# Finer gated-row sums, five early down-projection steps, and the second stage's stores on GpSimd's queue, in a one-core hybrid decoder layer

## The chip, the cores and the metric

The kernel runs on one core of one Trainium2 chip. Time is the device time of one execution in microseconds (us). The core has five engines with instruction streams of their own: TensorE (PE; its weight loads are PEld), VectorE (DVE), ScalarE (ACT), GpSimd (POOL) and SyncE (SP). In this kernel DMA transfers are issued by SP and by POOL; each works through its own stream in order.

## The reference

One decoder layer over 2048 tokens of width 1024, all float32: a mixer of two recurrent head groups, then a convolutional feed-forward block with a feed-forward width of 2816, and a final norm. Cut to what matters here:

```python
def _conv_ffn(h, w_up, conv_w, conv_b, w_down):
    u = h @ w_up                                # 1024 -> 5632
    u = lax.conv_general_dilated(u, conv_w[:, None, :], window_strides=(1,),
            padding=[(CONV_WIDTH - 1, 0)], ...) + conv_b     # causal, 3 taps, per column
    gate, val = jnp.split(u, 2, axis=-1)
    return (jax.nn.silu(gate) * val) @ w_down   # 2816 -> 1024

def reference(x, ...):
    ...                                         # h, the two mixers o_hg and o_rw
    x = x + jnp.concatenate([o_hg, o_rw], axis=-1) @ w_out[l]
    x = x + _conv_ffn(_rmsnorm(x, norm2_w[l]), w_up[l], conv_w[l], conv_b[l], w_down[l])
    return _rmsnorm(x, final_norm_w)
```

## The kernel before

**Matmuls.** Every float32 operand is split into a high part (written by ScalarE, a CAST; L245 in `split`) and a low part (the difference, written by DVE; L246). A product is three matmuls: high by high (L261), low by high (L262), high by low (L263). Names ending in h and l are these parts: uraw is a raw up-projection weight and uwh, uwl its parts; draw is a raw operand of the down-projection, and dah, dal, dbh, dbl the parts of its two sides.

**Stages.** Stage 1, up to about 1388 us, holds the input projections and the mixers; the change doesn't touch it. The second stage begins with the output projection of the last of four token blocks (its rows go to the DRAM tensor x1d, L1227). Then come the up-projection, until about 2337 us, and the down-projection, until the end.

**Up-projection** (`run`). It is done for the two halves of the tokens (h = 0, 1; 1024 tokens each) and for 22 pairs of column blocks (NFF = 22), so 44 iterations n. One iteration computes a gate and a value block of 128 columns as a 2x2 block product with seven products instead of eight (the Strassen-Winograd scheme): `prod` issues 12 matmuls of 128x512, seven times. The left operands are the weight quarters and their sums (s1 to s4); the right ones are the blocks Bh, Bl of the normed input and their sums Ts. ScalarE copies intermediate sums (m1, m2, m3), DVE adds and applies the convolution (L1431 to L1440), ScalarE applies the silu and DVE multiplies (L1445). The result y, 128 rows by 1024 tokens, is stored as two 256 KB pieces to the DRAM tensors gd0 and gd1 (first half) or gd2 and gd3 (second half) at L1447. The last two products of an iteration and all that follows (`late`) run inside the next iteration. The last iteration's `late` also calls `down_start`.

**Side work.** Between the products, `aside(n)` takes one entry of a list of small steps per product, not before the iteration that the entry names (`first_at`). The list holds, in this order: the norm of the last two token blocks (`norm_last`, with stores to h2d), the sums Ts of the second half, the sums Tw of the down weights, the sums Sg0 of the rows gd0 and gd1 (g = 0; 11 of them, KH = 11) and eight sums Sg1 of gd2 and gd3 (g = 1; EARLY = 8). Each sum loads four 128x512 tiles into a ring of six buffers (br), does four additions on DVE in place (L1280, L1281 in one step, L1283, L1284 in a second, for the gated rows; L1271 to L1275 for the others) and stores four tiles (L1266). `four` spreads this over five entries: loads, nothing, two operations, two operations and all four stores, nothing.

**Down-projection.** Also 2x2 with seven products, per half g; one step is a pair of 128-row operands and 12 matmuls (`d_matmuls`), and `steps` lists 143 of them. The accumulators are da and db. One product (fa) runs between the two halves of the up-projection and its result waits in M2. `down_start` runs the first three steps with the up-projection's buffers (br and uwh, uwl) inside the last `late`, ahead of the work on the last y, so that TensorE has these 36 matmuls while y and the silu are computed. Then the loop loads four steps ahead (draw, a ring of six tiles, three steps), splits two steps ahead (`take`), and issues the matmuls; some steps also load a tile of x1d (xt3), and steps 13, 19 and 25 call `g_sums` for the three remaining sums Sg1 (sraw, stores at L200). The finished rows go to the output at L1489.

**What sets the order.** Before the change every DMA of the second stage is issued by SP, except for the two stores of the last y, which POOL issues. Within an engine a scheduler orders the instructions by their dependences and by a list of priorities that follows the code, so a step may stand earlier in an engine's order than the code has it. Tiles of a pool are reused in rings, and whoever writes such a tile waits for the last reader.

Of the kernel before, what the change touches and what calls it, by code (L numbers as in the profile page):

```python
# [18 lines left out]
P = 128  # L19
# [42 lines left out]
def tile_layer(ctx, tc, consts, x, norm1_w, w_in, hg_lb_logits, hg_norm_w, rw_shift_mu, rw_w0, rw_w2,  # L62
# [4 lines left out]
    V, S, TE = nc.vector, nc.scalar, nc.tensor  # L67
    dma = nc.sync.dma_start

# [122 lines left out]
    def g_sums(tile_, g, kk):  # L192

        a11, a12, a21, a22 = (tile_(krows(gd_[2 * g + u], q, kk)) for u in range(2) for q in range(2))
        V.tensor_add(a22, a21, a22)
        V.tensor_sub(a21, a11, a21)
        V.tensor_sub(a11, a22, a11)
        V.tensor_sub(a12, a12, a11)
        for i, t_ in enumerate((a22, a11, a21, a12)):
            dma(krows(Sg[g][i], 0, kk), t_)  # L200

# [906 lines left out]
    with ExitStack() as c2:  # L1108
# [36 lines left out]
        with tc.tile_pool(name="op", bufs=1, reuse_waits="tile") as op_:  # L1145
# [52 lines left out]
            for dh in range(2):  # L1198
# [26 lines left out]
                for i in range(4):  # L1225
                    V.tensor_add(xt[i], accs[i], xt[i])
                    dma(x1d[b][i * P:(i + 1) * P, dh * 512:dh * 512 + 512], xt[i])  # L1227


        with tc.tile_pool(name="up", bufs=1, reuse_waits="tile") as up:  # L1230
# [11 lines left out]
            def norm_last(b, i2):  # L1242
# [11 lines left out]
                def evict(k, tp, w):  # L1254
                    t_ = hr.tile([P, 256], F32, tag="br", name="h2", bufs=6)
                    act(t_, tp, AF.Copy, scale=w)
                    dma(h2d[b][k * P:(k + 1) * P, i2 * 256:i2 * 256 + 256], t_)

# [17 lines left out]

            def s_make(ts, part):
                a11, a12, a21, a22 = ts
                if part == 0:
                    V.tensor_add(a22, a21, a22)  # L1280
                    V.tensor_sub(a21, a11, a21)  # L1281
                else:
                    V.tensor_sub(a11, a22, a11)  # L1283
                    V.tensor_sub(a12, a12, a11)  # L1284
# [3 lines left out]
            s_out = lambda row: lambda ts: [(row(i), ts[j]) for i, j in enumerate((3, 0, 2, 1))]  # L1288
            for b in (2, 3):
# [30 lines left out]
            def between():  # L1320
# [10 lines left out]
                for i in range(4):  # L1331
                    t_ = raw_(None)
                    act(t_, accs[i], AF.Copy)
                    dma(M2[i], t_)
                yield
# [8 lines left out]
            def run():  # L1344
# [9 lines left out]
                for n in range(2 * NFF + 1):  # L1354
# [41 lines left out]
                    if late is not None:  # L1396
                        late(end=down_start) if n == 2 * NFF else late()
                    if n == 2 * NFF:
                        break
                    cg = up.tile([P, 16 + 2 * BLK], F32, tag="cg", name="cg", bufs=2)[:, 0:2 + 2 * BLK]  # L1400
# [21 lines left out]
                    def late(h=h, fb=fb, operand=operand, prod=prod, acc_a=acc_a, acc_d=acc_d, a22=a22, a12=a12, cg=cg,  # L1422
# [23 lines left out]
                        for b in range(2):  # L1446
                            (dma if end is None else nc.gpsimd.dma_start)(gd_[2 * h + b][fb * P:(fb + 1) * P, :],  # L1447
                                                                  ys[0][:, b * BLK:(b + 1) * BLK])
# [4 lines left out]
    with tc.tile_pool(name="dn", bufs=1, reuse_waits="tile") as dn:  # L1453
# [10 lines left out]
        raws = {}  # L1464

        def load(s_):
            if s_ < N and s_ not in raws:
                g, p, kk = steps[s_]
                raws[s_] = d_loads(s_, d_raw("draw"))
                if p == 0 and kk in (4, 6, 8, 10) or p == 2 - g and kk in (1, 3, 5, 7):  # L1470
                    u, i = (0, kk // 2 - 2) if p == 0 else (1, kk // 2)
                    t_ = dn.tile([P, D], F32, tag="xt3", name="xt3", bufs=12)
# [32 lines left out]
        accs = {"a": dstate["accs"]}  # L1505
        for s_ in range(3, 7):
            load(s_)
        take(3)
        take(4)
# [3 lines left out]
        for s_ in range(3, N):  # L1513
            g, p, kk = steps[s_]
# [60 lines left out]
```

## Time and profile before

| what | value |
|---|---|
| median of 3 runs | 2748.41 us |
| the three runs | 2748.82, 2748.41, 2739.77 us |
| the profiled execution | 2740.67 us |
| its span, first to last instruction | 2738.9 us |
| granted TensorE clock, mean | 0.989 |
| TensorE busy in the span | 2634.9 us, 96% |
| DVE, ScalarE, GpSimd busy | 69%, 49%, 13% |

The profiled execution is close to the fastest of the runs. Rows of the timeline give the start, the duration, the engine, the line of the code, the operation and "out<-in" tiles; the bracket at the end says how long the engine had been idle and what ended that. SPq are the DMA instructions that SP issues. Rows of waits give the waiting instruction, what it waited for, and the total, the number of times and the longest. A matmul lasts 0.39 us but a new one starts every 0.23 us, since they overlap.

### The profile page before, as it was taken

The page shows a single profiled execution, that of the slowest core. Times are in us where ns is not written, and L with a number is a line of the kernel's source. Part 1 is how long each engine was busy: PE and PEld are TensorE (multiplying, and loading weights), DVE is VectorE, ACT ScalarE, POOL GpSimd, SP SyncE. Part 2 cuts the span into 40 slices and gives each one's busy share as a digit, 9 for nine tenths or more (in the row PEclk, how much of TensorE's full clock was granted, in tenths as well). Part 3 has the DMA queues.
Part 4 walks back from the last instruction along what each step waited for, and adds up shares of the span by engine and source line. Part 5 has one row for each costly group of instructions (what it writes and reads, how often), then busy time and mean ns, then how long its engine had stood idle before and what let it go on. Part 6 is the DMA issues. An engine that isn't in the chain of part 4 may idle for free.

```text
span 2738.9 us, 47949 instructions
## 1 busy us (share of the span) xinstructions
PE 2634.9 (96%) x18059; PEld 2098.9 (77%) x18059; DVE 1896.9 (69%) x3665; ACT 1344.5 (49%) x2168; POOL 367.4 (13%) x660
## 2 busy tenths in 40 slices
PE   7999999989999999999899999999999999999998
PEld 6777777767777767777677788887888877788887
DVE  4857656566556664656667889988898888667556
ACT  5446443444544444334456754556545444445444
POOL 6433222212321113222100000000000000000000
PEclk9999999999999999999999999999999999999999
DMA  8655544355663546844575357746763454888665
GB/s 302 200 159 165 165 138 128 115 152 164 216 189 105 152 137 208 273 142 133 168 260 179 118 197 265 237 151 208 259 223 123 145 185 151 285 303 273 214 193 185
DMA packets 365438, 517.87 MB, mean 189 GB/s; under 512 B 97440, under 2 KB 194070, under 8 KB 365206
## 3 DMA queue, kind: packets, MB, share of 16 engines
q1 hardware_dynamic: 313265, 345.39, 39.3%
q0 software_dynamic: 51872, 169.41, 19.0%
q8 instruction: 142, 2.33, 0.3%
q14 instruction: 91, 0.74, 0.1%
q10 hardware_dynamic: 68, 0.02, 0.0%
HBM read 376.27 MB, written 138.41 MB: 188 GB/s over the span
## 4 chain that ended last, share of the span: by engine, by line
PE 67%; DMA 10%; DVE 10%; issue 6%; ACT 4%; SPq 1%; POOL 1%; DVEq 0%; ACTq 0%; POOLq 0%
PE pj L261 8%; PE pj L262 7%; PE pj L263 7%; PE ua L261 4%; PE ua L263 4%; PE ua L262 4%; PE da L262 2%; PE da L261 2%; PE da L263 2%; PE ud L263 2%; PE ud L261 2%; PE ud L262 2%; PE db L262 2%; PE db L263 2%; PE hg L972 2%
## 5 line engine op out<-in xcount | busy, mean ns | idle before, releaser
L261 PE MATMUL pj<-hh,wh 128*128 128x512 f32 x960 | 403.2, 420 | 2.3 <-ACT hh L117 1.4
L263 PE MATMUL pj<-hh,wl 128*128 128x512 f32 x960 | 380.0, 396 | 0.1
L262 PE MATMUL pj<-hl,wh 128*128 128x512 f32 x960 | 379.1, 395 | 0.0
L261 PE MATMUL ua<-Bh,uwh 128*128 128x512 f32 x704 | 277.0, 393 | 10.4 <-ACT m L117 9.3
L263 PE MATMUL ua<-Bh,uwl 128*128 128x512 f32 x704 | 274.5, 390 | 0.1
L262 PE MATMUL ua<-Bl,uwh 128*128 128x512 f32 x704 | 274.2, 390 | 0.0
L261 PEld LDWEIGHTS pj<-hh,wh 128*128 128x128 f32 x960 | 181.7, 189 | 55.4 <-issue 12.7
L263 PEld LDWEIGHTS pj<-hh,wl 128*128 128x128 f32 x960 | 181.5, 189 | 40.8 <-DMA wl<-Win170l 0.9
L262 PEld LDWEIGHTS pj<-hl,wh 128*128 128x128 f32 x960 | 181.8, 189 | 39.6 <-issue 6.2
L245 ACT CAST uwh<-uraw 128x512 fp32r<-128x512 f32 x220 | 133.2, 616 | 101.5 <-PE ua L262 42.0
L246 DVE TENSOR_TENSOR dal<-draw,dah 128x512 fp32r<-128x512 f32 x140 | 96.7, 690 | 116.0 <-ACT dah L245 115.4
L245 ACT CAST dah<-draw 128x512 fp32r<-128x512 f32 x140 | 87.1, 622 | 169.9 <-PE da L262 81.6
L246 DVE TENSOR_TENSOR uwl<-uraw,uwh 128x512 fp32r<-128x512 f32 x220 | 146.8, 686 | 31.3 <-ACT uwh L245 31.1
L261 PEld LDWEIGHTS ua<-Bh,uwh 128*128 128x128 f32 x704 | 132.2, 188 | 41.8 <-ACT m L117 14.0
L263 PEld LDWEIGHTS ua<-Bh,uwl 128*128 128x128 f32 x704 | 132.2, 188 | 28.7 <-DVE uwl L246 1.0
L262 PEld LDWEIGHTS ua<-Bl,uwh 128*128 128x128 f32 x704 | 132.3, 188 | 26.6
L261 PE MATMUL ud<-Bh,uwh 128*128 128x512 f32 x352 | 137.8, 391 | 0.0
L263 PE MATMUL ud<-Bh,uwl 128*128 128x512 f32 x352 | 137.1, 389 | 0.0
L262 PE MATMUL ud<-Bl,uwh 128*128 128x512 f32 x352 | 137.0, 389 | 0.0
L261 PE MATMUL da<-dbh,dah 128*128 128x512 f32 x340 | 131.2, 390 | 3.4 <-ACT dbh L245 3.4
L262 PE MATMUL da<-dbl,dah 128*128 128x512 f32 x340 | 132.5, 390 | 0.5 <-DVE dbl L246 0.5
L263 PE MATMUL da<-dbh,dal 128*128 128x512 f32 x340 | 132.1, 389 | 0.0
(570 smaller groups left out, 6049.5 us busy)
## 6 DMA issues: line engine op xcount, KB each, us to landing
uraw<-in_w_up_dram SPq DMA_DIRECT2D x176, 256.0 KB, 3.2
woraw<-in_w_out_dram POOLq DMA_DIRECT2D x96, 256.0 KB, 3.6
br<-gd SPq DMA_DIRECT2D x90, 256.0 KB, 4.4
draw<-Sg SPq DMA_DIRECT2D x88, 256.0 KB, 3.2
draw<-Tw SPq DMA_DIRECT2D x88, 256.0 KB, 3.5
gd<-y SPq DMA_DIRECT2D x86, 256.0 KB, 3.0
Sg<-br SPq DMA_DIRECT2D x76, 256.0 KB, 2.5
xt<-x1d SPq DMA_DIRECT2D x32, 512.0 KB, 6.7
```

The lines of the kernel that those rows point to most:

```text
L245: S.copy(hi, src)
L246: V.tensor_sub(lo, src, hi.bitcast(F32))
L261: TE.matmul(acc, lh, rh, start=first, stop=False, skip_group_check=skip)
L262: TE.matmul(acc, lh, rl, start=False, stop=False, skip_group_check=skip)
L263: TE.matmul(acc, ll, rh, start=False, stop=last, skip_group_check=skip)
L972: TE.matmul(o, kt[:, t0:t0 + 64], qs, start=True, stop=True, tile_position=(0, e * 64))
```

## The change

The change has five parts.

1. `store`, a DMA issued by GpSimd, takes over the stores of the second stage: x1d of the last block, h2d, Ts, Tw, Sg, all of gd, M2, and the output rows of the first half (g = 0). The eight output tiles of the second half stay on SP, as do all loads.
2. The sums of the gated rows are made by a new function, `sums`, with seven entries: loads, nothing, nothing, and then one operation with its own store in each of four. A sum of the second half may start one iteration later (KH + 2 + kk for KH + 1 + kk).
3. Seven instead of eight sums of the second half run in the up-projection (EARLY = 7); four instead of three in the down-projection, at steps 13, 19, 25 and 31.
4. `down_start` runs five steps instead of three (DS = 5), and their loads are no longer all written ahead of them. The loop starts at step 5.
5. The four x1d tiles of the first product are loaded at other steps (XT).

```diff
-    dma = nc.sync.dma_start
+    dma, store = nc.sync.dma_start, nc.gpsimd.dma_start
...
-    EARLY = 8
+    DS = 5
+    EARLY = 7
...
-            dma(krows(Sg[g][i], 0, kk), t_)
+            store(krows(Sg[g][i], 0, kk), t_)
...
-                    dma(x1d[b][i * P:(i + 1) * P, dh * 512:dh * 512 + 512], xt[i])
+                    store(x1d[b][i * P:(i + 1) * P, dh * 512:dh * 512 + 512], xt[i])
...
-                          lambda: make(ts, 0), lambda: (make(ts, 1), [dma(d, t_) for d, t_ in dsts(ts)]), None])
+                          lambda: make(ts, 0), lambda: (make(ts, 1), [store(d, t_) for d, t_ in dsts(ts)]), None])
...
+            def sums(g, kk):
+
+                ts = []
+                ops = ((3, V.tensor_add, 2, 3), (2, V.tensor_sub, 0, 2), (0, V.tensor_sub, 3, 0), (1, V.tensor_sub, 1, 0))
+
+                def op(d, f, a, b, i):
+                    f(ts[d], ts[a], ts[b])
+                    store(krows(Sg[g][i], 0, kk), ts[d])
+
+                aside_of([lambda: ts.extend(raw_(krows(gd_[2 * g + u], q, kk)) for u, q in QB), None, None]
+                         + [lambda o=o, i=i: op(*o, i) for i, o in zip((0, 2, 1, 3), ops)])
+
             for g in range(2):
-                for kk in range(({0: KH, 1: EARLY})[g]):
-                    first_at[0] = NFF + 1 + g * (KH + 1 + kk)
-                    four([krows(gd_[2 * g + u], q, kk) for u, q in QB], s_make,
-                         s_out(lambda i, g=g, kk=kk: krows(Sg[g][i], 0, kk)))
+                for kk in range((KH, EARLY)[g]):
+                    first_at[0] = NFF + 1 + g * (KH + 2 + kk)
+                    sums(g, kk)
...
-                raws = [d_loads(s_, raw_) for s_ in range(3)]
-                for s_ in range(3):
-                    lhs, rhs = (split(uw, t_, [P, BLK], "uw", 5) for t_ in raws[s_])
+                for s_ in range(DS):
+                    lhs, rhs = (split(uw, t_, [P, BLK], "uw", 5) for t_ in d_loads(s_, raw_))
...
-                            (dma if end is None else nc.gpsimd.dma_start)(gd_[2 * h + b][fb * P:(fb + 1) * P, :],
+                            store(gd_[2 * h + b][fb * P:(fb + 1) * P, :],
...
-                if p == 0 and kk in (4, 6, 8, 10) or p == 2 - g and kk in (1, 3, 5, 7):
+                if p == 0 and kk in XT or p == 2 - g and kk in (1, 3, 5, 7):
...
-            dma(out[0, t0:t0 + P, :], t_)
+            (dma if g else store)(out[0, t0:t0 + P, :], t_)
...
-        for s_ in range(3, 7):
+        for s_ in range(DS, DS + 4):
```

In order listings a row gives the line, the operation, "out<-in" with the tiles' numbers, and the size. Lines of the changed kernel are one to four higher (L1445 is L1447, L1280 to L1284 are L1293).

**A sum of the second half.** DVE before, from the product y to the first operation of the sum that loads y's rows (tiles br 22178 to 22184):

```order
L1445 TENSOR_TENSOR y0_22052<-y0_22052,y1_22057 128x1024
L246 TENSOR_TENSOR uwl_22206<-uraw_21984,uwh_22205 128x512
L246 TENSOR_TENSOR uwl_22241<-uraw_22155,uwh_22240 128x512
L1340 TENSOR_TENSOR s1_22257<-uraw_22157,uraw_22159 128x512
L1436 COPY cg_22236<-halo_15086 128x2
L1341 TENSOR_TENSOR s2_22258<-s1_22257,uraw_22153 128x512
L1415 TENSOR_TENSOR uraw_22157<-uraw_22153,uraw_22157 128x512
L1419 TENSOR_TENSOR cv_22066<-ud_22068,m3_22149 128x512
L246 TENSOR_TENSOR uwl_22262<-s2_22258,uwh_22261 128x512
L1420 TENSOR_TENSOR uraw_22155<-uraw_22155,s2_22258 128x512
L1436 COPY cv_22237<-halo_15086 128x2
L246 TENSOR_TENSOR uwl_22282<-s1_22257,uwh_22281 128x512
```

The next row before is the operation of L1280. And DVE after, from a y to the first operation of the sum that loads its rows (br 22232 to 22238; br 22063 belongs to the sum before it):

```order
L1447 TENSOR_TENSOR y0_21865<-y0_21865,y1_21870 128x1024
L1341 TENSOR_TENSOR s1_22070<-uraw_21966,uraw_21968 128x512
L247 TENSOR_TENSOR uwl_22046<-uraw_21964,uwh_22045 128x512
L1342 TENSOR_TENSOR s2_22071<-s1_22070,uraw_21962 128x512
L1417 TENSOR_TENSOR uraw_21966<-uraw_21962,uraw_21966 128x512
L1422 TENSOR_TENSOR uraw_21964<-uraw_21964,s2_22071 128x512
L247 TENSOR_TENSOR uwl_22075<-s2_22071,uwh_22074 128x512
L1421 TENSOR_TENSOR cv_21879<-ud_21881,m3_21958 128x512
L1293 TENSOR_TENSOR br_22063<-br_22063,br_22061 128x512
L1438 COPY cg_22041<-halo_15086 128x2
L1438 COPY cv_22042<-halo_15086 128x2
L247 TENSOR_TENSOR uwl_22093<-s1_22070,uwh_22092 128x512
```

The next row after is the first operation (br 22238). The distance of twelve rows from y to that operation is the same; what moved in between is the fourth operation of the sum before.

SP before, around the stores of the same y and the loads of its sum:

```order
L1447 DMA gd2_156<-y0_22052 128x512
L1447 DMA gd3_157<-y0_22052 128x512
L1140 DMA uraw_22326<-in_w_up_dram 128x4x128
L1123 DMA br_22180<-gd2_156 128x512
L1123 DMA br_22182<-gd3_157 128x512
L1123 DMA br_22184<-gd3_157 128x512
L1140 DMA uraw_22328<-in_w_up_dram 128x4x128
L1123 DMA br_22349<-gd2_156 128x512
L1266 DMA Sg10_162<-br_22184 128x512
```

SP after, at a later sum of the same kind:

```order
L1141 DMA uraw_22475<-in_w_up_dram 128x4x128
L1141 DMA uraw_22477<-in_w_up_dram 128x4x128
L1124 DMA br_22576<-gd2_156 128x512
L1124 DMA br_22578<-gd3_157 128x512
L1124 DMA br_22580<-gd3_157 128x512
L1124 DMA br_22745<-gd2_156 128x512
```

The stores are gone from SP (they stand on POOL, three Sg stores, two gd stores and the fourth Sg store per iteration), and an iteration's uraw loads now all stand ahead of the loads of the gated rows.

**The end of the up-projection.** DVE before, from the last gate rows to the first split of the down-projection's loop:

```order
L1440 TENSOR_SCALAR y1_23279<-cv_23084,cvt_14639,y1_23279 128x1024
L246 TENSOR_TENSOR uwl_23257<-br_23210,uwh_23256 128x512
L1439 TENSOR_SCALAR y0_23274<-cg_23083,cvt_14639,y0_23274 128x1024
L1440 TENSOR_SCALAR y0_23274<-cg_23083,cvt_14639,y0_23274 128x1024
L1445 TENSOR_TENSOR y0_23274<-y0_23274,y1_23279 128x1024
L246 TENSOR_TENSOR dal_23316<-draw_23295,dah_23315 128x512
```

The same place after:

```order
L1442 TENSOR_SCALAR y1_23311<-cv_23068,cvt_14639,y1_23311 128x1024
L247 TENSOR_TENSOR uwl_23241<-br_23234,uwh_23240 128x512
L247 TENSOR_TENSOR uwl_23261<-br_23256,uwh_23260 128x512
L1441 TENSOR_SCALAR y0_23306<-cg_23067,cvt_14639,y0_23306 128x1024
L247 TENSOR_TENSOR uwl_23265<-br_23258,uwh_23264 128x512
L247 TENSOR_TENSOR uwl_23285<-br_23280,uwh_23284 128x512
L1442 TENSOR_SCALAR y0_23306<-cg_23067,cvt_14639,y0_23306 128x1024
L247 TENSOR_TENSOR uwl_23289<-br_23282,uwh_23288 128x512
L1447 TENSOR_TENSOR y0_23306<-y0_23306,y1_23311 128x1024
L247 TENSOR_TENSOR dal_23350<-draw_23327,dah_23349 128x512
```

The four splits of the two added steps (br 23256 to 23282) stand ahead of the last y. On TensorE 60 matmuls of down steps with operands in br and uw stand ahead of the first one with dbh, where 36 stood; POOL issues 950 instructions instead of 664 in the whole program and SP 963 instead of 1249, 286 DMAs that moved.

More of the change, by code (lines that the diff above doesn't have):

```diff
@@ L1256, in evict @@
                     act(t_, tp, AF.Copy, scale=w)
-                    dma(h2d[b][k * P:(k + 1) * P, i2 * 256:i2 * 256 + 256], t_)
+                    store(h2d[b][k * P:(k + 1) * P, i2 * 256:i2 * 256 + 256], t_)
                 g = transposed(xt, "n2", lambda: pst("tp"), evict)
@@ L1275, in t_make @@
                     V.tensor_sub(b21, b21, b22)
[L1277 to L1284, printed above, removed]
             QB = [(q, b) for q in range(2) for b in range(2)]
             t_out = lambda row: lambda ts: [(row(i), ts[j]) for i, j in enumerate((0, 3, 1, 2))]
-            s_out = lambda row: lambda ts: [(row(i), ts[j]) for i, j in enumerate((3, 0, 2, 1))]
             for b in (2, 3):
@@ L1333, in between @@
                     act(t_, accs[i], AF.Copy)
-                    dma(M2[i], t_)
+                    store(M2[i], t_)
                 yield
@@ L1398, in run @@
                     if n == 2 * NFF:
+                        assert not side
                         break
@@ L1464, in tile_layer @@
         raws = {}
+        XT = (5, 6, 8, 9)
         def load(s_):
@@ L1469, in load @@
                 raws[s_] = d_loads(s_, d_raw("draw"))
[L1470 to L1471 removed]
+                if p == 0 and kk in XT or p == 2 - g and kk in (1, 3, 5, 7):
+                    u, i = (0, XT.index(kk)) if p == 0 else (1, kk // 2)
                     t_ = dn.tile([P, D], F32, tag="xt3", name="xt3", bufs=12)
@@ L1505, in tile_layer @@
         accs = {"a": dstate["accs"]}
-        for s_ in range(3, 7):
+        for s_ in range(DS, DS + 4):
             load(s_)
-        take(3)
-        take(4)
+        take(DS)
+        take(DS + 1)
         fw = dn.tile([P, D], F32, name="fw")
@@ L1512, in tile_layer @@
         sums_at = {KH + 6 * j + 2: EARLY + j for j in range(KH - EARLY)}
-        for s_ in range(3, N):
+        for s_ in range(DS, N):
             g, p, kk = steps[s_]
```

## The prediction

> **What bounds the kernel now.** I read the busy shares first, then the second stage cut into stretches, then what TensorE waits for, and last the timeline around those waits. The page's first lines and the table by stretch (columns: from and to, length, then busy time and instruction count of each engine, granted clock, DMA share, GB/s):
>
> ```profile
> PE 2634.9 (96%) x18059; PEld 2098.9 (77%) x18059; DVE 1896.9 (69%) x3665; ACT 1344.5 (49%) x2168; POOL 367.4 (13%) x660
> ...
> 1611.00:1858.00 247.00, 245.33 (x1083) 202.63 (x1083) 227.70 (x359) 126.14 (x187) 0.00 (x0) 1.00 0.68 223
> 1858.00:1921.00 63.00, 58.90 (x255) 47.09 (x254) 53.12 (x84) 41.18 (x68) 0.00 (x0) 1.00 0.64 204
> 1921.00:2146.00 225.00, 224.96 (x993) 186.02 (x992) 198.37 (x289) 115.00 (x169) 0.00 (x0) 1.00 0.58 188
> 2146.00:2330.00 184.00, 176.89 (x773) 144.23 (x773) 154.46 (x225) 87.09 (x128) 0.00 (x0) 1.00 0.53 172
> 2330.00:2410.00 80.00, 75.95 (x328) 60.83 (x327) 52.75 (x78) 36.99 (x57) 1.10 (x2) 1.00 0.83 289
> ```
>
> TensorE sets the time. The stretch 1921 to 2146 shows its pace with nothing in the way: 225 us for 993 matmuls, 0.2266 us each. At that pace the other stretches lose: 1611 to 1858, 247 − 1083 × 0.2266 = 1.6 us; 1858 to 1921, 5.2; 2146 to 2330, 8.8; 2330 to 2410, 5.7. The change removes no matmul and its edits begin at 1438 us, so it can only win back a part of these some 21 us, and a little before 1611. What TensorE waits for after 1388 us (total, times, longest), and the DVE wait behind the 8.8 us:
>
> ```profile
> PE ua L261 <- ACT m L117: 9.3, 8, 1.7
> PE da L261 <- ACT dbh L245: 3.4, 3, 1.5
> ...
> PE da L262 <- DVE dbl L246: 0.5, 2, 0.2
> ...
> DVE br L1280 <- DMA br<-gd: 24.3, 8, 3.9
> ```
>
> TensorE waits for ScalarE's eviction m, but m is late because the DVE order behind it stands still: 24.3 us before eight sums of gated rows (L1280). One such period, DVE's rows and then SP's:
>
> ```profile
> 2268.61 1.23 DVE L1445 TENSOR_TENSOR y<-y,y 128x1024 f32<-128x1024 f32 x1
> ...
> 2278.70 0.69 DVE L1280 TENSOR_TENSOR br<-br 128x512 f32<-128x512 f32 x1 [3.92 <-DMA br<-gd]
> ...
> 2284.23 0.69 DVE L1284 TENSOR_TENSOR br<-br 128x512 f32<-128x512 f32 x1
> 2284.84 1.28 DVE L1439 SCALAR_TENSOR_TENSOR y<-cg,cvt,y 128x1024 f32<-128x1024 f32 x1
> ...
> 2289.04 1.22 DVE L1445 TENSOR_TENSOR y<-y,y 128x1024 f32<-128x1024 f32 x1
> ...
> 2298.65 0.69 DVE L1280 TENSOR_TENSOR br<-br 128x512 f32<-128x512 f32 x1 [2.78 <-DMA br<-gd]
> ```
> ```profile
> 2269.86 0.82 SPq L1447 DMA_DIRECT2D gd<-y  x2
> 2272.27 0.38 SPq L1140 DMA_DIRECT2D uraw<-in_w_up_dram  x1
> 2272.74 1.88 SPq L1123 DMA_DIRECT2D br<-gd  x4
> ...
> L1280 DVE TENSOR_TENSOR br<-br x8: 691/692/694, 2156.7 to 2298.7; 128x512 f32<-128x512 f32 x8
> ```
>
> It is a loop. The product y ends at 2269.84, is stored, loaded back, and the first sum operation can start at 2278.70, 8.9 us later (8.4 in the next period); after that DVE runs without a gap until the next y. The period is (2298.7 − 2156.7) / 7 = 20.29 us, where 84 matmuls need 19.03: 1.26 us lost seven times is the 8.8.
>
> **The sums of the second half (g=1).** The diff starts each one iteration later, which by itself would take the loop apart. The order of the changed kernel shows that it doesn't: the first operation still stands twelve rows behind the y on whose store its loads wait, as before. Three things do change. First, the fourth operation (0.61 us by the step from 2284.23 to 2284.84) leaves the busy part of the loop and stands before the first operation, in the shadow of the 2.8 to 3.9 us wait: −0.61 per period. Second, seven sums run here instead of eight. Third, the stores go through GpSimd's queue. Its price in the second stage shows in one pair of stores, and in stage 1 in the 120 weight stores of L556; SP's stores of the same tensor in this stretch stand behind them (the last row of each fence is issue to landing: shortest, median, longest):
>
> ```profile
> 2344.84 1.22 DVE L1445 TENSOR_TENSOR y<-y,y 128x1024 f32<-128x1024 f32 x1 [1.13 <-ACT y L117]
> 2346.36 1.10 POOL L1447 DMA_DIRECT2D gd<-y  x2 [955.73 <-DVE y L1445]
> ...
> DMA to landing us min/median/max: 3.0/4.2/5.4
> ```
> ```profile
> L556 POOL DMA_DIRECT2D Win280h<-wh x1: 560/560/560, 8.4 to 8.4; - x1
> ...
> DMA to landing us min/median/max: 2.3/3.1/9.1
> ```
> ```profile
> L1447 SPq DMA_DIRECT2D gd<-y x20: 319/380/435, 2147.8 to 2328.7; - x20
> ...
> DMA to landing us min/median/max: 2.5/2.9/3.4
> ```
>
> POOL starts 0.30 us after y ends (2346.06 to 2346.36), where SP needs 0.02; the second store follows 0.55 later. So the second gd store is issued at y + 0.85 instead of + 0.43. With about 2.9 us to landing it is there at y + 3.75. That is hidden: SP issues the load that depends on it third, at 2272.74 + 2 × 0.47, y + 3.84, because an uraw load in front of it waits for the operation of L1415 until y + 2.43, and in the changed order an uraw load still stands there. Only the first load, bound to the first store (y + 0.30 + 2.9 = 3.2 against 2.9 now), moves the loop, by +0.3. If the landing takes the 4.2 of the POOL pair, the delay is 0.85 + 4.2 − 3.84 = +1.2; with its 5.4, +2.4. I take +0.3, since this stretch has a DMA share of 0.53 and the pair landed in one of 0.83. Period: 20.29 − 0.61 + 0.3 = 19.98, 0.95 us lost in the six periods between seven sums = 5.7 instead of 8.8: **−3**. Ends: −8.8 if the wait vanishes; 6 × (20.29 − 0.61 + 2.4 − 19.03) = 18.3 instead of 8.8, +9.5, at 5.4.
>
> **The passage to the down-projection.** The last y, and the silu before it, delay the first split of the down steps (ScalarE's, TensorE's and SP's rows):
>
> ```profile
> 2343.75 1.06 ACT L117 ACTIVATE y<-y 128x1024 f32<-128x1024 f32 x1 [3.06 <-DVE y L1440]
> 2345.22 0.61 ACT L245 CAST dbh<-draw 128x512 fp32r<-128x512 f32 x1
> ```
> ```profile
> 2343.98 0.39 PE L263 MATMUL da<-uwh,uwl 128*128 128x512 f32 x1
> 2345.89 1.19 PE L261 MATMUL da<-dbh,dah 128*128 128x512 f32 x4 [1.51 <-ACT dbh L245]
> ...
> 2392.97 1.19 PE L261 MATMUL da<-dbh,dah 128*128 128x512 f32 x4 [1.48 <-ACT dbh L245]
> ```
> ```profile
> 2346.69 0.32 SPq L1460 DMA_DIRECT2D draw<-gd  x1
> ...
> 2385.38 2.98 SPq L200 DMA_DIRECT2D Sg<-sraw  x4
> ```
>
> Now TensorE has 36 matmuls of early down steps after the up-projection and has used them up at 2344.2. With five early steps it has 60, 5.4 us more, until about 2349.6. ScalarE has its dbh of 2345.22 ready at 2345.83; the four casts of the two added steps (0.62 each, the row's form) fall in the wait of 3.06 before the silu, and DVE's four splits (0.61 each, 2.4 us) stand before the last y, which then ends up to 2.4 us later, at 2348.5 at worst. That still beats 2349.6 or misses it by well under 1 us, so the 1.51 and the small waits after it (0.5 together) go; their successors come about 2 us earlier against need, since SP, whose next load now goes out at 2346.69 only, has no stores in front of the loads any more. At 2392.97 TensorE waits for loads that SP issued behind four stores of a late sum (2385.38, behind their DVE operations); these stores are GpSimd's now. But the DMA share here is 0.83, and loads that are issued earlier only help if the transfers have room; a fourth late sum (8 more transfers of 256 KB, each some 0.75 us at the 350 GB/s or so of a full queue, the estimate from 0.83 ↔ 289) comes on top, in part later than 2410, where TensorE had slack. I take −4.5 of the 5.7; ends −2.5 (the first wait alone, with its restart) and −5.7.
>
> **The rest.** At 1453 TensorE waits because four x1d stores stand on SP ahead of the loads of Ts:
>
> ```profile
> 1453.81 0.50 PE L261 MATMUL ua<-Bh,uwh 128*128 128x512 f32 x1 [1.01 <-ACT uwh L245]
> ```
> ```profile
> 1438.96 2.11 SPq L1227 DMA_DIRECT2D x1d<-xh  x4
> 1441.18 2.73 SPq L1123 DMA_DIRECT2D br<-Ts  x4
> ```
> ```profile
> br<-in_w_down_dram SPq DMA_DIRECT2D x46, 256.0 KB, 4.3
> ...
> Tw<-br SPq DMA_DIRECT2D x44, 256.0 KB, 3.5
> ```
>
> Without the 2.11 us of stores the 1.01 goes: −1.2 with its restart (ends 0 and −1.2). The T sums (1611 to 1858) reuse a buffer after its store: store, load, operation, 3.5 + 4.3 us now. The order leaves nine such chains with 5.1 to 5.7 us of DVE work between, where before they had 5.7 to 8.1. Up to 0.5 us more wait in each is 4.5 us of DVE time; DVE has 247 − 227.7 = 19 us free there, so little reaches TensorE: +1 (0 to +5). For 1858 to 1921 I take −0.5 (0 to −2): shorter queues on SP, same engines waiting. The sums of the first half get a whole iteration of distance and stay hidden. The stores cost POOL about 286 × 0.55 = 157 us, on an engine that shows x0 in all stretches before 2330; the out stores of g=0 and the M2 stores have no waiter near.
>
> **Sum:** −3 − 4.5 − 1.2 + 1 − 0.5 = −8.2. The profiled execution took 2740.67 us (span 2738.9 and 1.8 around it), so 2732.5 by its measure. It is near the lowest of the runs shown (2739.77); the median is 2748.41, 7.7 above it. Against that median: 2740.2.
>
> **The rivals.**
> *All waits go.* If the loop of the second half opens (the loads of a sum land before DVE reaches it), 8.8 + 5.7 + 1.2 and 2 of the 5.2 are won: −17.7, 2730.7. Against it speaks the order: same y, same distance. Chance 0.16.
> *GpSimd's stores land late.* The mechanism on the other side: between y and the sums, and in the nine T chains, a store's landing L stands in series. The loop changes by 6 × (0.65 + L + 0.85 − 3.84) − 8.8, the chains cost about 9 × (L − 3.0), if DVE's slack doesn't take it. At L = 4.2 that is +2.4 and +10.8, less 6.2 of the passage, 1453 and the rest, together +7; at 5.4, +9.6 + 21.6 − 6.2 = +25. It turns the sign from an L of about 3.75 on. For it: the only pair in this stage. Against: the 3.1 of L556. Time 2755 to 2773. Chance 0.13.
> *GpSimd's stores wait for DVE.* If a store can't be set going while DVE is busy, landings go to the 9.1 that L556 shows at most: the same formulas give +32 and +55, less 6.2: about 2829. The median of 3.1 beside a working DVE speaks against it. Chance 0.05. The Trainium skill (page "SBUF — State Buffer", section "SBUF: two separate sides") states such a rule: while DVE runs a two-port fast-mode operation, as an fp32 copy does, GpSimd can't write its descriptors and the transfer seems blocked; the advice is to issue from SP or ACT. By that rule this change would be a mistake, if the TENSOR_TENSOR and SCALAR_TENSOR_TENSOR forms that fill DVE here counted as such; no run here shows that yet.
> *Nothing comes of it.* The passage's loads are held by the transfers themselves, and the loop keeps its length: −2 to +1, 2747. Chance 0.14.
>
> **The numbers.** The likeliest case has 0.52, with its own range from its ends of −16 to +1: 2732 to 2749. 0.5% is 13.7 us, about what a measurement of this kernel tells from no change: 2734.7 to 2762.1 is "same". Faster by more: most of the first rival and the low end of the likeliest, 0.27. Slower by more: two thirds of the late stores, all of the third, and 0.03 for what I don't see, 0.17. The range takes in the first rival's middle and the late stores up to about +10: 2724 to 2759.
>
> **What would show it.** In the changed profile: no wait of da for dbh near 2346; none or less than 1 us near 2390; SP rows without gaps for stores; DVE's wait before the first sum operation of the second half still 2 to 4 us, seven times, at a period of 19.7 to 20.3; POOL's gd<-y landing at a median near 3. Wrong would be: a landing over 3.7, DVE waits in 1611 to 1858 well over 12 us, or a loop without its wait.

## The result and the profile after

The changed kernel takes 2759.57 us (median of 6 runs, 2752.26 to 2763.86) against 2744.89 us for the kernel before in the same comparison (median of 6 runs, 2739.77 to 2748.82). The ratio is 1.0058, with a 95% interval of 1.0041 to 1.0076: 0.6% slower, some 16 us. Forecast was 2740.2, 8.2 us below the median of the three runs of before that were known then (2748.41) and 4.7 below the median here.

The profiled execution took 2755.66 us, its span is 2753.9, 15.0 more than before. The busy shares of its page and the stretches that the prediction looked at (columns as before; the same places of the program stand 7 to 21 us later than before):

```profile
PE 2645.0 (96%) x18059; PEld 2105.3 (76%) x18059; DVE 1896.2 (69%) x3665; ACT 1343.6 (49%) x2168; POOL 522.3 (19%) x946
...
1611.00:1858.00 247.00, 238.10 (x1043) 194.21 (x1042) 218.47 (x343) 119.38 (x177) 47.45 (x88) 1.00 0.66 214
...
2146.00:2330.00 184.00, 175.54 (x766) 142.78 (x766) 150.97 (x221) 86.92 (x128) 24.80 (x46) 1.00 0.51 165
2330.00:2410.00 80.00, 79.78 (x351) 65.17 (x350) 55.57 (x81) 39.59 (x60) 5.37 (x10) 1.00 0.67 237
```

In 1611 to 1858 TensorE gets through 40 matmuls fewer than before in the same time; in 2330 to 2410 it now runs almost without a gap. The same in TensorE's waits over the whole span, after:

```profile
PE ua L262 <- ACT m L117: 22.3, 17, 4.5
...
PE da L263 <- DVE dbl L247: 0.2, 1, 0.2
```

The waits of da for dbh (3.4 us) are gone. The waits of ua for the eviction m have gone from 9.3 us to 22.3, from 8 to 17 of them, and the longest is 4.5 instead of 1.7.

To see where, I add up TensorE's waits over 0.25 us by place in the program, in the one profiled execution of each kernel. The experiments are in the table too; they are told below. "Early" is from the first up-projection matmul to the eighth y (the norms of the last blocks), "T" from there to the nineteenth y (T sums), "fa" the stretch between the halves, "g=1" the second half up to the first down step, "down" all behind it.

| kernel | early | T | fa | g=1 | down | all |
|---|---|---|---|---|---|---|
| before | 2.5 | 1.7 | 4.0 | 7.1 | 3.4 | 18.7 |
| after | 6.9 | 8.9 | 4.8 | 8.5 | 0.0 | 29.1 |
| e1 five down steps alone | 2.4 | 0.0 | 3.9 | 6.7 | 2.2 | 15.1 |
| e2 after, all stores on SP | 0.7 | 0.0 | 4.3 | 4.7 | 2.4 | 12.2 |
| e3 before, stores on GpSimd | 7.9 | 7.8 | 4.2 | 9.5 | 2.1 | 31.6 |
| e4 after, T stores on SP | 6.3 | 0.0 | 6.0 | 6.4 | 0.6 | 19.2 |
| e5 after, last tile loaded last | 8.2 | 7.8 | 4.5 | 9.8 | 0.0 | 30.3 |
| e6 as e4, and x1d on SP | 5.6 | 0.6 | 4.3 | 8.5 | 0.3 | 19.4 |
| e7 as e2, all g=1 sums late | 1.0 | 2.0 | 3.7 | 0.0 | 14.9 | 21.6 |
| e8 gd and Sg stores on GpSimd | 3.0 | 0.5 | 3.4 | 8.4 | 2.5 | 17.9 |
| e9 as e2, late Sg on GpSimd | 2.1 | 0.0 | 4.2 | 6.3 | 0.0 | 12.6 |
| e10 as e2, T stores on GpSimd | 0.9 | 6.5 | 3.9 | 5.7 | 1.9 | 18.8 |
| e11 as e2, x1d on GpSimd | 4.3 | 1.7 | 5.4 | 4.2 | 2.1 | 17.7 |
| e12 as e2, h2d on GpSimd | 3.2 | 0.3 | 3.6 | 6.0 | 2.1 | 15.1 |

Before to after: early +4.4, T +7.2, fa +0.8, g=1 +1.4, down −3.4, together +10.4. The other 4.6 of the 15.0 fit the granted clock. Before, it is 1.00 from 1420 to 2730 us; after, it falls to 0.94 in 1440 to 1470, 0.83 in 1560 to 1570 and 0.89 in 1885 to 1900 (rows at the end), together some 5 us of full speed. The expectations of the later experiments count the same losses by windows of time, which gives up to 1.3 us more than this table.

**The T sums.** DVE's waits between 1611 and 1858, before and then after:

```profile
DVE br L1271 <- DMA br<-h2d: 3.6, 2, 2.6
...
DVE br L1272 <- DMA br<-h2d: 1.0, 1, 1.0
DVE br L1272 <- DMA br<-in_w_down_dram: 0.8, 2, 0.5
DVE br L1271 <- DMA br<-in_w_down_dram: 0.4, 1, 0.4
```
```profile
DVE br L1272 <- DMA br<-in_w_down_dram: 5.7, 3, 2.3
DVE br L1273 <- DMA br<-h2d: 5.6, 2, 4.3
DVE br L1273 <- DMA br<-in_w_down_dram: 5.5, 3, 2.0
```

5.8 us of waits for loads have become 16.8, in eight places. (Before has one more wait there, 1.5 us at 1723.08, for which the trace names no releaser.) One of them, by DVE's, POOL's and SP's rows of the changed kernel:

```profile
1688.92 0.69 DVE L1273 TENSOR_TENSOR br<-br 128x512 f32<-128x512 f32 x1
...
1694.54 0.69 DVE L247 TENSOR_TENSOR uwl<-uraw,uwh 128x512 fp32r<-128x512 f32 x1
1697.24 0.69 DVE L1273 TENSOR_TENSOR br<-br 128x512 f32<-128x512 f32 x1 [2.01 <-DMA br<-in_w_down_dram]
```
```profile
1689.90 0.54 POOL L1267 DMA_DIRECT2D Tw<-br  x1 [1.34 <-DVE br L1273]
```
```profile
1692.04 5.15 SPq L1124 DMA_DIRECT2D br<-in_w_down_dram  x3
```

The operation ends at 1689.61, its store starts at 1689.90, a load into the same buffer goes out when the store has landed, and the next sum's operation starts at 1697.24: 7.6 us. DVE has 5.6 us of work in between and stands for 2.0. TensorE feels it a little later, as m comes late. From the landing times of the DMAs, the chains behind the other waits take 6.9 to 7.9 us (10.3 at 1635 and 9.2 at 1677): 0.3 to POOL's start, 2.5 to 3.9 to the store's landing (6.7 at 1635), 3.1 to 4.6 for the load where it is recorded. Those of the down weights before took 6.8 to 8.8 us and cost 0.5 at most. So most chains have not become longer; DVE comes to their end sooner. In DVE's order seven chains have only 5.0 to 6.1 us of other work inside, where before a single one had 5.7 and the rest 6.9 or more.

**The wait near 1449.** SP's, ScalarE's and TensorE's rows after:

```profile
1442.47 0.98 SPq L1141 DMA_DIRECT2D uraw<-in_w_up_dram  x2
```
```profile
1448.31 0.62 ACT L246 CAST uwh<-uraw 128x512 fp32r<-128x512 f32 x1 [1.73 <-DMA uraw<-in_w_up_dram]
1448.84 0.59 ACT L117 ACTIVATE m<-ua 128x512 f32<-128x512 f32 x1
```
```profile
1449.48 0.50 PE L262 MATMUL ua<-Bh,uwh 128*128 128x512 f32 x1 [4.47 <-ACT m L117]
```

SP issues these uraw loads at 1442.47; before they went out at 1449.03, behind the x1d stores and the loads of h2d. In ScalarE's order the cast of that load has moved ahead of the eviction m, and the load lands 5.8 us after its issue. The eviction, whose input is ready, stands behind a cast that waits. Before, ScalarE evicted m at 1442.08, ahead of that cast.

**The passage.** As forecast: no wait of da for dbh near 2346, 2358 or 2393.

### The profile page after: what moved, and what is told of

Read it like the earlier page. It is cut to its first block, busy times and chain, and to the rows that moved or that the text cites. A ratio compares the mean times of both kernels' runs of the same rounds, so it can differ in the third digit from the quotient of the medians.

```text
span 2753.9 us, 48228 instructions
## 1 busy us (share of the span) xinstructions
PE 2645.0 (96%) x18059; PEld 2105.3 (76%) x18059; DVE 1896.2 (69%) x3665; ACT 1343.6 (49%) x2168; POOL 522.3 (19%) x946
## 4 chain that ended last, share of the span: by engine, by line
PE 70%; DMA 9%; DVE 9%; issue 6%; ACT 4%; POOL 1%; SPq 1%; DVEq 0%; POOLq 0%; ACTq 0%
PE pj L262 8%; PE pj L263 7%; PE pj L264 7%; PE ua L262 4%; PE ua L264 4%; PE ua L263 4%; PE da L262 3%; PE da L263 3%; PE da L264 3%; PE ud L263 2%; PE ud L264 2%; PE ud L262 2%; PE db L264 2%; PE db L262 2%; PE db L263 2%
## 5 line engine op out<-in xcount | busy, mean ns | idle before, releaser
L262 PE MATMUL ua<-Bh,uwh 128*128 128x512 f32 x704 | 279.0, 396 | 22.3 <-ACT m L117 22.3
L1449 POOL DMA_DIRECT2D gd<-y x88 | 47.5, 544 | 492.9 <-DVE y L1447 449.3
```

The costliest lines, as they stand in the source:

```text
L262: TE.matmul(acc, lh, rh, start=first, stop=False, skip_group_check=skip)
L1449: store(gd_[2 * h + b][fb * P:(fb + 1) * P, :], ys[0][:, b * BLK:(b + 1) * BLK])
```

## The experiments

Two theories stood after this reading. A: the stores on GpSimd make the loss, and the early steps and finer sums are a gain. B: the new places of the sums and loads make it, whoever issues the stores. All kernels were timed against the kernel before on the same chip; the profiled executions come from several chips and differ in stage 1 by up to 7 us from before, so the table compares only what lies behind it.

**e1, e2, e3: the parts apart.** e1 takes the early steps alone:

```diff
-                raws = [d_loads(s_, raw_) for s_ in range(3)]
-                for s_ in range(3):
-                    lhs, rhs = (split(uw, t_, [P, BLK], "uw", 5) for t_ in raws[s_])
+                for s_ in range(DS):
+                    lhs, rhs = (split(uw, t_, [P, BLK], "uw", 5) for t_ in d_loads(s_, raw_))
...
-        for s_ in range(3, 7):
+        for s_ in range(DS, DS + 4):
```

> The kernel before with part 4 and 5 of the change alone: five early down steps and the x1d loads at other steps; all stores stay on SP. Theory A (the passage is won, the queue costs): the waits of da for dbh at 2345.9, 2358.1 and 2393.0 (3.4 us idle, about 4 with the restarts) go, 3 to 5 us faster, ratio 0.998 to 0.999. Theory B (the early steps displace other work and cost as much as they win): within 1 us of before.

e2 is the changed kernel with its stores on SP:

```diff
-    dma, store = nc.sync.dma_start, nc.gpsimd.dma_start
+    dma, store = nc.sync.dma_start, nc.sync.dma_start
...
-                            store(gd_[2 * h + b][fb * P:(fb + 1) * P, :],
+                            (dma if end is None else nc.gpsimd.dma_start)(gd_[2 * h + b][fb * P:(fb + 1) * P, :],
```

> The changed kernel with every store back on SP (the last y's two stores on GpSimd, as before): finer sums and five early steps without the queue. Theory A (GpSimd's queue makes the loss): faster than before by 4 to 8 us; DVE's waits before the T sums back at 7 us or less, no wait of 4 us near 1449. Theory B (the new places of the sums and loads make it): still 8 to 16 us slower than before.

e3 is the kernel before with `store` in the eight kinds of places of part 1 of the change, and nothing else.

> The kernel before with the stores on GpSimd's queue and nothing else. Theory A: slower than before by 12 to 22 us, the changed kernel's loss plus what the passage won; DVE waits before the T sums of 14 us or more, and the 4 us wait near 1449. Theory B: within 4 us of before.

Measured: e1 2734.48 us, ratio 0.9994 (0.9976 to 1.0012); e2 2732.99 us, ratio 0.9985 (0.9969 to 1.0001); e3 2759.03 us, ratio 1.0082 (1.0062 to 1.0102). e3 alone is some 22 us slower than before, the upper end of what A expected and no less than the whole change, and its early and T losses are the changed kernel's: theory A holds. e2's gain, 4 us, is at the lower end of what A expected, and its interval just touches no change. In e1 the waits near 2346 and 2358 went (1.9 us together); the one near 2393 stayed and grew from 1.5, here in e1 and e2 (TensorE's waits from 2335 to 2430):

```profile
PE da L262 <- ACT dbh L246: 2.2, 1, 2.2
```
```profile
PE da L262 <- ACT dbh L246: 2.4, 1, 2.4
```

So early steps alone win 1.2 us of waits in the passage, not 3 to 5; the time of e1 can't be told from before. In the changed kernel the wait near 2393 is gone as well, and e9 asks why.

**e4: the T sums' stores back on SP**, in the changed kernel:

```diff
-                          lambda: make(ts, 0), lambda: (make(ts, 1), [store(d, t_) for d, t_ in dsts(ts)]), None])
+                          lambda: make(ts, 0), lambda: (make(ts, 1), [dma(d, t_) for d, t_ in dsts(ts)]), None])
```

> The changed kernel with only the T sums' stores (Ts and Tw, 60 of them) back on SP. Theory A in its narrow form (a T sum's chain of store, load, operation got longer): the some 8 us lost between 1641 and 1810 go, so 6 to 10 us faster than the changed kernel, 6 to 10 slower than before. If the loss there comes from the other stores' leaving SP: no more than 2 us better than the changed kernel.

2740.97 us, ratio 1.0018 (1.0005 to 1.0030), 11 us better than the changed kernel by the ratios. No wait of TensorE is left in the T stretch. Narrow A holds, with somewhat more than was expected.

**e10: the reverse**, all stores on SP but these 60.

> All stores on SP but the 60 of the T sums, which GpSimd issues. If they alone make the loss at the T sums: TensorE loses 5 to 10 us between 1620 and 1830 (0.0 with all stores on SP), ratio 1.001 to 1.004, DVE waits before the T sums of 10 us or more. If the loss needs the other stores' absence from SP too: below 3 us.

2744.70 us, ratio 1.0008 (0.9990 to 1.0026), 0.0023 above e2 as ratios stand, 6 us, though the two intervals overlap. In the trace TensorE waits 6.5 us in the T stretch, where e2 has none. TensorE's and DVE's waits there:

```profile
PE ua L262 <- ACT m L117: 6.5, 6, 1.7
```
```profile
DVE br L1273 <- DMA br<-h2d: 5.0, 1, 5.0
DVE br L1273 <- DMA br<-in_w_down_dram: 5.0, 4, 2.3
DVE br L1272 <- DMA br<-in_w_down_dram: 4.4, 3, 1.6
```

In the table every kernel with these 60 stores on GpSimd loses 6.5 to 8.9 us there and every one with them on SP 2.0 at most: the 60 stores make that loss by themselves. The ratio came out a little below what was expected.

**e5: is it the short distance in DVE's order?** All stores stay on GpSimd; each T sum loads last the tile that it needs last:

```diff
+                def loads():
+                    b11, b12, b22, b21 = (raw_(srcs[i]) for i in (0, 1, 3, 2))
+                    ts.extend((b11, b12, b21, b22))
+
-                aside_of([lambda: ts.extend(raw_(v) for v in srcs), None,
-                          lambda: make(ts, 0),
+                aside_of([loads, None, lambda: make(ts, 0),
```

> The changed kernel, all its stores on GpSimd, with one edit: a T sum loads the tile that only its fourth operation reads last instead of third. In DVE's order this leaves three chains store, load, operation with 5.7 us of other DVE work in between, where the changed kernel has seven with 5.1 to 6.1. Theory D (the loss at the T sums comes from the short distance in DVE's order, the queue being no slower): TensorE's loss between 1620 and 1830 falls from 10.2 us to 3 to 6, 4 to 7 us faster than the changed kernel. Theory Q (GpSimd's queue is slow by itself): no more than 2 us faster.

2761.84 us, ratio 1.0058 (1.0036 to 1.0081): no faster than the changed kernel. The T loss is 7.8 us instead of 8.9, in three waits instead of eight, and one of them is 4.5 us long, behind the longest DVE wait of that stretch:

```profile
1691.30 0.68 DVE L1280 TENSOR_TENSOR br<-br 128x512 f32<-128x512 f32 x1
1696.76 0.69 DVE L1276 TENSOR_TENSOR br<-br 128x512 f32<-128x512 f32 x1 [4.78 <-DMA br<-in_w_down_dram]
```

The order left three chains with 5.7 to 5.8 us of other work inside, as expected, but they take 7.5, 8.5 and 10.5 us. In the rows above the operation of 1696.76 waits for a load behind the store of the fourth operation of the sum two before it: that operation ended at 1686.23, its store started at 1686.53 and landed at 1690.55, the load went out at 1690.57. DVE's waits for the T sums' loads are 17.0 us in all, as many as in the changed kernel (16.8). Fewer short chains, each waited for longer, cost the same. The time is the one that theory Q gave, but the run doesn't show that the queue is what made these chains long. That the loss comes from waits for the chain store, load, operation is shown by e4 and e10; how much of it is the order and how much GpSimd's 0.3 us later start and 0.1 to 0.3 us later landing (medians after: Tw 3.6, Ts 4.0; before 3.5 and 3.7) stays open, as no kernel has the one without the other. A larger ring than six buffers, which would lengthen the distance, wasn't tried.

**e6, e11, e12: the early loss.** e6 is e4 with x1d on SP too; e11 and e12 are e2 with x1d alone, or h2d alone, on GpSimd.

> The changed kernel with the T sums' stores and the four x1d stores of the last block on SP. If the x1d stores' leaving SP makes the wait of 4.5 to 5 us near 1449 (SP then issues uraw loads earlier, and ScalarE's order has the cast of that load ahead of the eviction m): that wait goes, 4 to 6 us faster than with the T stores alone on SP, within 2 us of before. If the wait has another cause: as slow as with the T stores alone, ratio about 1.002.

> All stores on SP but the x1d stores of the last block, on GpSimd. If they make the loss before 1611 (7.2 us in the changed kernel, 0.8 with all stores on SP): 4 to 6 us lost near 1449. If not: below 2.5 us there, and the ratio as with all stores on SP.

> All stores on SP but the 32 of h2d, on GpSimd. With x1d back on SP the loss before 1611 stayed at 6.2 us, with h2d back too it fell to 3.5. If h2d makes it: 3 to 6 us lost before 1611. If not: below 2 us.

e11: 2742.91 us, ratio 0.9993 (0.9978 to 1.0008); early 4.3, nearly all of it the wait near 1449, with the same rows (3.74 behind the cast of uraw). x1d on GpSimd is enough to make it. e6: 2740.04 us, ratio 0.9992 (0.9972 to 1.0011), which overlaps with e4's 1.0018; in its trace the wait of 4.8 that e4 has is gone, but two of 1.25 and 2.44 stand in the same place, and the early loss is 5.6 instead of 6.3. Its expectation was half wrong: the time came out as expected, and the order of that wait changes, but the loss in the trace mostly stays. e12: 2739.37 us, ratio 0.9984 (0.9968 to 1.0001), early 3.2. The kernels with both kinds of stores on SP scatter from 0.7 to 3.0 us there (before, e1, e2, e7, e8, e9, e10), so the sum doesn't tell what h2d costs. One wait does, that of the transposes (tp) near 1555, here in e11 and e12:

```profile
PE tp L256 <- DVE xt L1253: 0.6, 1, 0.6
```
```profile
PE tp L256 <- DVE xt L1253: 1.5, 1, 1.5
```

It is 0.6 to 1.1 us in the eight kernels with h2d on SP and 1.5 to 3.1 in the six with h2d on GpSimd. So h2d costs about 1 us there; through which chain wasn't looked into.

**e8: the loop of the second half.** Only the stores of gd and of the early gated-row sums are on GpSimd.

> The changed kernel with only the stores of gd and of the gated rows' sums in the up-projection on GpSimd, all others on SP. If the queue lengthens the loop of the second half: TensorE's waits at 2146 to 2330 are 2 to 4 us above the 5.3 with all stores on SP. If the landing is hidden behind the uraw load, as the prediction had it: within 1 us of that.

2741.46 us, ratio 0.9990 (0.9972 to 1.0008). TensorE's and DVE's waits from 2146 to 2330 in e2, then in e8:

```profile
PE ua L262 <- ACT m L117: 4.9, 5, 1.3
...
DVE br L1293 <- DMA br<-gd: 21.1, 7, 3.6
```
```profile
PE ua L262 <- ACT m L117: 8.4, 6, 1.6
...
DVE br L1293 <- DMA br<-gd: 25.2, 7, 4.6
```

3.5 us more wait of TensorE: the queue lengthens the loop, by 0.6 us for each of seven sums. These are single executions that scatter: in the table's g=1 column the five kernels with the new sums and gd on SP (e2, e9 to e12) have 4.2 to 6.3 us, the five with gd on GpSimd (after, e4, e5, e6, e8) 6.4 to 9.8, on average 2.9 more. The rows of POOL and the landings show from what: the second gd store goes out 0.83 us after y instead of 0.42, lands 2.6 us later (before 2.9), and the load that waits for it goes out 0.4 to 0.5 us behind that, after the loads ahead of it. From y to the first operation it takes 9.24 us on average in e8, 8.66 in e2, 8.47 before.

**e7: no early sums of the second half** (EARLY = 0 in e2; all eleven in the down-projection).

> All stores on SP, five early steps, finer sums, and none of the second half's sums in the up-projection: all eleven run in the down-projection (steps 13, 19 and so on to 73). If the loop of y, store, load and sum makes the loss at 2146 to 2330, it goes (5 to 8 us) and the time is 4 to 8 us below that of all stores on SP with seven early sums, ratio about 0.996. Rival: the down-projection has no room for 88 more transfers; TensorE waits for draw there and the gain is lost, ratio 0.998 or more.

2753.91 us, ratio 1.0037 (1.0021 to 1.0054). The loop is the cause of the g=1 loss (0.0 us left there), and the rival was right about the outcome: the gain is lost in the down-projection. From 2440 to 2570, before and then e7:

```profile
2440.00:2570.00 130.00, 130.00 (x575) 107.67 (x574) 84.58 (x126) 66.67 (x129) 0.00 (x0) 1.00 0.79 265
```
```profile
2440.00:2570.00 130.00, 116.50 (x467) 90.68 (x466) 88.92 (x133) 60.56 (x114) 0.00 (x0) 0.93 0.92 322
```

The DMA share rises from 0.79 to 0.92, and TensorE waits 13.5 us for operands. That the transfers have no room is not shown by this alone. SP also stands 28 us for DVE there, before the stores of the late sums, with loads behind them; the longest of SP's waits in e7:

```profile
SPq L201 <- DVE sraw L196: 19.3, 6, 6.0
```

Which of the two makes TensorE's waits isn't settled; late sums with their stores on GpSimd were not tried with EARLY = 0.

**e9: one kind of store on GpSimd**, in e2:

```diff
-            store(krows(Sg[g][i], 0, kk), t_)
+            nc.gpsimd.dma_start(krows(Sg[g][i], 0, kk), t_)
```

> All stores on SP, finer sums and five early steps, as in the run with all stores on SP, and one kind of store on GpSimd: those of the late sums in the down-projection (L201, 16 of them). The changed kernel has no wait at 2393, all stores on SP has one of 2.4 us. If those 16 stores on SP hold up the loads behind them: the wait at 2393 goes or falls below 1 us, 1 to 3 us faster than with all stores on SP, ratio 0.996 to 0.998. If not: as all stores on SP, about 0.9985.

2733.92 us (2729.67 to 2737.58), ratio 0.9963 (0.9944 to 0.9981): faster than the kernel before and than the changed one; against e2 the intervals overlap. TensorE's waits from 2335 to 2430 are

```profile
PE da L263 <- DVE dbl L247: 0.2, 1, 0.2
```

The wait near 2393 was SP's: four stores that wait for DVE held up the loads behind them (2385.38 in the rows of before). In every kernel with these stores on SP (before, e1, e2, e8, e10, e11, e12) TensorE waits 1.5 to 2.4 us near there, in every one with them on GpSimd (after, e3, e4, e5, e6, e9) 0.6 at most. That is the one place where GpSimd's queue pays.

## Why the prediction was wrong

- **The passage: right in kind and size.** −3.4 us of waits against −4.5 forecast (ends −2.5 and −5.7). Of it the early steps make 1.2, since the wait near 2393 grew, and the Sg stores' move the rest (e1, e9), so the two shares were the other way round.
- **The T sums: the step that failed.** "Up to 0.5 us more wait in each is 4.5 us of DVE time; DVE has 247 − 227.7 = 19 us free there, so little reaches TensorE: +1 (0 to +5)." Measured: 1.3 to 4.3 us in each of eight places, 11 us of DVE waits more, and 7.2 us of TensorE, above the end of +5. The first half of the error: the prediction saw the distance fall from 5.7 to 8.1 us down to 5.1 to 5.7, and gave no working for the 0.5. Its own rows gave a price: 0.3 + 3.5 + 4.3 is 8.1 us of chain against 5.1 to 5.7 of cover, 2.4 us and more each. The second half: an idle share of DVE is no cover for a wait that stands in DVE's order ahead of what feeds the next eviction. The prediction's own sign of being wrong, DVE waits well over 12 us in 1611 to 1858, came true: 16.8 before the T sums alone.
- **The place at 1453: wrong in sign.** Forecast −1.2, measured +4.4 for the early stretch, 3.5 of it in the wait near 1449 that stands in place of the 1.0 at 1453. The step reckoned with the loads of Ts coming earlier and didn't look at ScalarE's order, in which the earlier uraw load drew its cast ahead of the eviction m.
- **The loop: wrong in sign, from two terms.** Without the queue the prediction's figures give 6 × 0.65 = 3.9 us of loss instead of 8.8, −4.9. The finer sums and one sum fewer won less: with the stores on SP the waits are 7.1 and 6.7 us in the two kernels with the old sums (before, e1) and 4.2 to 6.3 in the five with the new ones, some −1.5 on average. For GpSimd's queue +0.3 in each of six periods, 1.8, was reckoned; measured is 3.5 (e8 against e2), or 2.9 between the two groups of five. In all +1.4 came of the −3. The period is 20.8 us in the changed kernel (first operations from 2176.1 to 2300.9) and 20.1 in e2, where 19.98 was forecast. The landing was not late, 2.6 us; the 0.4 us of later issue and the loads ahead of the waiting one did it.
- **The rivals.** The other side was right, and it was given 0.13. Its mechanism, a store's later landing in series with the sums, was right about the place (T chains and loop) and wrong about the size that decides: the change is slower at landings of 2.6 us (gd) and 3.6 (Tw), below the 3.75 from which it was to turn; only Ts, a quarter of the chains' stores, is above it at 4.0. The rival that stores can't be set going while DVE is busy is refuted: in the rows of 1689 the store starts 0.29 us after its operation, with DVE at work on the next ones, and gd's 88 stores on GpSimd land in 2.6 us on median, with DVE at 69% of the span. By the rule on DVE and GpSimd in the Trainium skill (page "SBUF — State Buffer", section "SBUF: two separate sides") the stores would have had to wait if the operations that fill DVE here were of the two-port fast mode; the trace shows no such wait for these TENSOR_TENSOR and SCALAR_TENSOR_TENSOR forms.
- **Added up in TensorE's waits**, the −8.2 forecast became +10.4: the T sums are off by 6.2, the early stretch by 5.6, the loop by 4.4, the stretch between the halves by 1.3 and the passage by 1.1. So the T sums are the largest miss, but with them as forecast the change would still have been slower.
- The range ended at 2759.0, and the median is 2759.57. The likeliest case was given −16 to +1 "from its ends", but the upper ends of its own terms add up to +12 (9.5 − 2.5 + 0 + 5 + 0).

## What to carry to other kernels

Before a store moves to another queue, list every buffer that is loaded again behind it, and set the whole chain (operation, store, landing, load) against the work that stands in between in the new order, not against the change of one link. Moving DMAs also reorders engines that issue none of them: look at what now stands ahead of each eviction. A queue of its own pays for stores that wait for an engine while loads stand behind them, and here for no others.

## What the runs showed of the hardware that I had not expected

**A wait of 4 us costs more than itself.** Granted TensorE clock from 1440 to 1470 us (third column from the end), e2, then after, then e4:

```profile
1440.00:1470.00 30.00, 30.00 (x133) 24.34 (x132) 25.34 (x40) 22.21 (x38) 0.00 (x0) 1.00 0.62 200
```
```profile
1440.00:1470.00 30.00, 25.53 (x106) 20.66 (x105) 21.91 (x38) 18.09 (x30) 2.16 (x4) 0.94 0.65 220
```
```profile
1440.00:1470.00 30.00, 25.18 (x98) 20.20 (x97) 20.47 (x36) 16.56 (x27) 1.30 (x3) 0.89 0.52 178
```

The five kernels with one wait of 3.7 to 5.0 us near 1449 (after, e3, e4, e5, e11) have a clock of 0.89 to 0.94 there, and e6, with 1.25 and 2.44 close together, 0.94; all eight without have 1.00. At 0.94 and 0.89 these 30 us lose another 1.8 to 3.3 us of full speed. The Trainium skill (page "TensorE: Matmul & The Clock Gate", section "Part 1: The HAM clock gate (the "warmup" mystery)") says that the array's clock is halved after an idle window of about 3.4 us; the runs agree with that for waits of 3.7 us and more.

They also show it at less: for the pair in e6, and in the changed kernel behind single waits of 1.94 us at 1561.0 and 1.70 us at 1889.6:

```profile
1560.00:1570.00 10.00, 9.00 (x36) 7.16 (x37) 6.54 (x14) 5.85 (x12) 2.67 (x5) 0.83 0.54 170
...
1885.00:1900.00 15.00, 13.08 (x50) 10.13 (x49) 11.11 (x20) 8.96 (x17) 0.00 (x0) 0.89 0.85 290
```

Not every wait of that size does it. Before, one of 1.91 us at 1902.9 leaves the clock at 1.00:

```profile
1900.00:1915.00 15.00, 12.97 (x57) 10.09 (x56) 11.45 (x18) 6.22 (x10) 0.00 (x0) 1.00 0.40 130
```

**GpSimd's stores of gd land no later than SP's; others do.** Medians from issue to landing in the second stage, on SP (before) and then on GpSimd (after): gd 3.0 and 2.6 us, Tw 3.5 and 3.6, Ts 3.7 and 4.0, the early Sg 2.5 and 3.2, h2d 1.8 and 2.6, the late Sg 2.4 and 4.9, x1d 3.2 and 6.5. Of SP's stores the trace records the landing of a quarter or fewer (24 of 86 for gd, 2 of 8 for x1d), of GpSimd's that of all. What else was in transfer also differs, so the queue is not shown to be the cause. The rows of gd and x1d, before and then after:

```profile
gd<-y SPq DMA_DIRECT2D x86, 256.0 KB, 3.0
...
x1d<-xh SPq DMA_DIRECT2D x8, 256.0 KB, 3.2
```
```profile
gd<-y POOLq DMA_DIRECT2D x88, 256.0 KB, 2.6
...
x1d<-xh POOLq DMA_DIRECT2D x8, 256.0 KB, 6.5
```

What GpSimd adds ahead of that is 0.3 us from the operation's end to the store's start, where SP takes 0.03, and 0.54 us between two stores in place of 0.4.
